# Where the first FFN's gated banks are emptied, and which stage sums the second FFN's shift and scale

## The chip, the core and the metric

The kernel runs on one core of one Trainium2 chip. The engines named here are TensorE (PE, matmuls and transposes into the eight PSUM banks), VectorE (DVE), ScalarE (ACT), GpSimd (POOL) and SyncE (SP), whose queue issues the weight loads. Each engine works through a list of instructions that is fixed when the kernel is built; it takes them in that order and waits where one is not ready. The metric is the device time of one execution in microseconds, the median of several runs.

## The reference

A decoder trunk of two layers over one sequence of 256 tokens, width 1024, all in float32. A vector `c` modulates every sub-layer: for each layer nine vectors of length 1024 come out of one product, and each of them is a shift, a scale or a gate.

```python
for l in range(DEPTH):
    mod = cond @ ada_w[l] + ada_b[l]
    (sh1, sc1, g1, sh2, sc2, g2, sh3, sc3, g3) = jnp.split(mod, N_MOD, axis=-1)
    n1 = modulate(rmsnorm(h, norm_ffn1[l]), sh1, sc1)
    h = h + MACARON_WEIGHT * g1[:, None, :] * swiglu(n1, ffn1_w_gu[l], ffn1_w_down[l])
    n2 = modulate(rmsnorm(h, norm_mix[l]), sh2, sc2)
    h = h + g2[:, None, :] * hybrid_mixer(n2, positions, ...)
    n3 = modulate(rmsnorm(h, norm_ffn2[l]), sh3, sc3)
    h = h + MACARON_WEIGHT * g3[:, None, :] * swiglu(n3, ffn2_w_gu[l], ffn2_w_down[l])
return rmsnorm(h, final_norm)
```

`swiglu` is silu of one half of `x @ w_gu` times the other half, then `@ w_down` (2816 hidden columns). `hybrid_mixer` projects the tokens once and runs three groups of heads, A (dilated windows), B (latent attention) and C (attention over the 64 best keys that an indexer picks for each token), and projects their joined outputs with `w_out`.

## The kernel before

**Products.** The 256 tokens are two tiles of 128 rows. A float32 product is made of three products of halves: `split` copies a weight into `hi` (ACT, L243) and subtracts that from the weight into `lo` (DVE, L244), activations are split likewise, and PE adds hi x hi, lo x hi and hi x lo (L196). Chunks of gated activations are called `chh` and `chl`.

**The stream of weights.** Every weight is in one stream in DRAM, in order of use. `load` (L225) issues it from SP's queue, mostly 1 MB at a time, into `raw`, which has three buffers. A buffer comes free when DVE has made its last `lo` from it, or its last sum (below). `hi` and `lo` have six buffers each; the weights of the last two down blocks go to larger ones, `xhi` and `xlo`.

**The stages.** Each layer is an FFN, the mixer and a second FFN. The first FFN of the first layer has 11 blocks of 256 hidden columns. `lead` does its first four (LEADB) at once, k by k, in all eight PSUM banks (four named `pb`, four named `pa`), while the weights and the modulation arrive. It then applies silu (ACT, L642) and the product (DVE, L644) to each bank, transposes the results on PE (L201, `pb<-ident,pr`) and copies them as chunks (ACT L709, DVE L710). Blocks 4 to 10 follow one by one in `block`: `gu_mm` for each of the two halves f, then `gu_act` (ACT, DVE, then POOL's product L721 and POOL's `chl` L723). The down products of the blocks run behind, by the table FIRST_DOWN, in the four `pa` banks: before block 4 the first of them already runs.

**The modulation vectors.** The class `Ada` makes one vector in four steps, each a load of 1 MB and two DVE instructions that add a column of `cond` times a part of it to `acc` (L433 for the first, L435 for the others). `acc` has one buffer, so the next vector cannot begin before the former is used up. At the end a gate (names with G) is split and spread over the partitions by PE with `ones_r`; a shift or scale (SH, SC) takes eight PE transposes into two banks (`pb<-ident,acc`) and two DVE reductions (L460). ADA_PLAN says which vectors are made in which stage (layer 0: first FFN, mixer, second FFN, then layer 1), and `Jobs.run` spreads the steps over the blocks of the FFN (7 parts) or over eight places `j0` to `j7` in the list STEPS of the mixer. SC2 and SH2 are needed by the mixer's norm, G2 at the mixer's end, SC3 and SH3 by the second FFN's norm.

**The mixer.** The indexer of group C finds its keys by a chain of DVE maxima (L938, L939) that ends in the mask `msk` (L942). Head A's score products (`pb<-k,q`) and softmax (`neg`, L1031; `pe`) run beside and after it. Then come C's scores, which begin with the mask (`pb<-msk,identr`), and the output projection (`pa<-hi,chh` and so on) with G2 at the end.

**The order.** A scheduler lists the instructions by a simulated time, with a priority (`tc.high_priority`) for the steps that hand chunks on. What it lists, the chip keeps.

## Time and profile before

| | us |
|---|---|
| median of three runs (1097.83, 1098.70, 1100.39) | 1098.70 |
| the profiled execution | 1097.09 |
| its span in the trace | 1095.2 |
| PE busy in the span | 1049.6 |
| DVE busy | 819.8 |
| ACT busy | 620.1 |
| POOL busy | 194.9 |

The stages of layer 0 lie at these times of the trace: `lead` until 64.7, blocks 4 to 10 of the first FFN until 234.3, the mixer until 372.2, then the second FFN. Rows of a profile give the busy time of an engine, the mean length of one instruction in ns (one can overlap the next, so starts can be closer together than lengths), and the idle time ahead of a group of instructions with its releaser, the engine and line that ended the wait. [...]

### The profile page before, as it was taken

What the parts mean: (1) busy time and instruction counts of PE and PEld (TensorE: products, weight loads), DVE (VectorE), ACT (ScalarE), POOL (GpSimd) and SP (SyncE); (2) the same over time, 40 slices, a digit from 0 to 9 for tenths busy, and PEclk for the clock granted to TensorE, in tenths of its full rate; (3) what the DMA queues carried; (4) which work ended last, traced back from release to release, by engine and by line L of the source; (5) the groups of instructions that cost most, each with busy time, mean ns of one, the idle gap of its engine ahead of it and who ended that gap; (6) DMA issues with size and microseconds to landing.
All of it is one profiled execution on the core that took longest, in us unless ns stands there. A gap on an engine that the chain in (4) does not pass through costs nothing.

```text
span 1095.2 us, 15506 instructions
## 1 busy us (share of the span) xinstructions
PE 1049.6 (96%) x5634; PEld 878.2 (80%) x5634; DVE 819.8 (75%) x1334; ACT 620.1 (57%) x1177; POOL 194.9 (18%) x211
## 2 busy tenths in 40 slices
PE   5999999789999999999999999999999999999997
PEld 3778877668887688888878888887788778888885
DVE  6987877886795787786889877886669757656563
ACT  5554534366666766455555555555676667555561
POOL 1002221122000022232311323131200001222231
PEclk9999999899999999999999999999999999999999
DMA  8978887865355188787848888783536516666541
GB/s 340 373 267 296 293 320 269 334 223 189 111 188 193 64 298 290 270 303 267 293 160 303 292 303 293 281 313 132 188 125 208 178 58 210 233 227 224 212 183 38
DMA packets 38988, 255.84 MB, mean 234 GB/s; under 512 B 4824, under 2 KB 5208, under 8 KB 11008
## 3 DMA queue, kind: packets, MB, share of 16 engines
q1 hardware_dynamic: 38160, 253.14, 63.4%
q0 software_dynamic: 752, 1.71, 0.4%
q8 instruction: 44, 0.72, 0.3%
q14 instruction: 32, 0.26, 0.1%
HBM read 253.76 MB, written 1.07 MB: 233 GB/s over the span
## 4 chain that ended last, share of the span: by engine, by line
PE 80%; issue 6%; DVE 4%; ACT 4%; DMA 3%; POOL 2%; SPq 0%; DVEq 0%; POOLq 0%; ACTq 0%
PE pb L196 41%; PE pa L196 36%; PE pb L201 3%; DMA raw<-in_stream_dram 2%; DVE lo L244 1%; ACT hi L243 1%; DVE up L657 1%; PE pa L201 1%; POOL pr L721 1%; DMA invt<-in_inv_dram 1%; DVE acc L435 1%; POOL chl L723 1%; DMA scr<-gtab 0%; ACT nT L533 0%; ACT z L533 0%
## 5 line engine op out<-in xcount | busy, mean ns | idle before, releaser
L244 DVE TENSOR_TENSOR lo<-raw,hi 128x1024 fp32r<-128x1024 f32 (+3 forms) x314 | 380.7, 1227 | 145.5 <-ACT hi L243 143.5
L243 ACT CAST hi<-raw 128x1024 fp32r<-128x1024 f32 (+3 forms) x314 | 317.7, 1034 | 200.7 <-PE pb L196 94.0
L196 PE MATMUL pb<-nT,hi 128*128 128x512 f32 x1184 | 420.1, 396 | 5.3 <-ACT hi L243 5.3
L196 PE MATMUL pb<-nT,lo 128*128 128x256 f32 x1184 | 333.1, 284 | 2.2 <-DVE lo L244 2.2
L196 PEld LDWEIGHTS pb<-nT,hi 128*128 128x128 f32 x1184 | 222.9, 189 | 56.5 <-ACT hi L243 6.8
L196 PEld LDWEIGHTS pb<-nT,lo 128*128 128x128 f32 x1184 | 224.0, 189 | 6.1 <-DVE lo L244 3.1
L435 DVE SCALAR_TENSOR_TENSOR acc<-raw,cond,acc 128x1024 f32<-128x1024 f32 x118 | 155.5, 1317 | 20.1 <-DMA raw<-in_stream_dram 18.0
L721 POOL TENSOR_TENSOR pr<-sil,pr 128x256 f32<-128x256 f32 x74 | 76.8, 1038 | 516.4 <-DVE pr L718 310.6
L196 PE MATMUL pa<-hi,chh 128*128 128x512 f32 x328 | 105.0, 396 | 0.0
L196 PE MATMUL pa<-lo,chh 128*128 128x512 f32 x328 | 104.6, 392 | 0.4 <-DVE lo L244 0.4
L196 PE MATMUL pa<-hi,chl 128*128 128x512 f32 x328 | 103.3, 393 | 0.0
L196 PE MATMUL pa<-hi,nT 128*128 128x512 f32 (+3 forms) x320 | 89.2, 368 | 2.5 <-ACT nT L561 1.6
L723 POOL TENSOR_TENSOR chl<-pr,chh 128x256 fp32r<-128x256 f32 x74 | 81.7, 1105 | 53.6 <-ACT chh L723 53.6
L196 PEld LDWEIGHTS pa<-lo,chh 128*128 128x128 f32 x328 | 61.6, 189 | 13.5 <-DVE lo L244 0.8
L196 PEld LDWEIGHTS pa<-hi,chl 128*128 128x128 f32 x328 | 61.5, 189 | 13.1 <-issue 0.3
L196 PEld LDWEIGHTS pa<-hi,chh 128*128 128x128 f32 x328 | 60.3, 189 | 13.9 <-ACT chh L723 0.9
L196 PEld LDWEIGHTS pa<-hi,nT 128*128 128x128 f32 x320 | 58.8, 188 | 12.4 <-ACT nT L561 2.2
L196 PE MATMUL pa<-nT,hi 128*128 128x256 f32 x352 | 67.2, 289 | 0.0
L723 ACT CAST chh<-pr 128x256 fp32r<-128x256 f32 x74 | 30.0, 406 | 50.0 <-POOL pr L721 49.6
L196 PE MATMUL pb<-hi,nT 128*128 128x512 f32 x160 | 49.7, 413 | 8.4 <-ACT hi L243 3.9
L196 PEld LDWEIGHTS pa<-nT,hi 128*128 128x128 f32 x352 | 54.7, 189 | 3.3 <-issue 3.1
L196 PE MATMUL pa<-lo,nT 128*128 128x512 f32 (+3 forms) x160 | 54.2, 367 | 0.0
(210 smaller groups left out, 1278.2 us busy)
## 6 DMA issues: line engine op xcount, KB each, us to landing
raw<-in_stream_dram SPq DMA_DIRECT2D x218, 1024.0 KB, 4.9
up<-in_stream_dram SPq DMA_DIRECT2D x16, 512.0 KB, 12.6
raw<-in_stream_dram SPq DMA_DIRECT2D x4, 976.0 KB, 4.7
raw<-in_stream_dram SPq DMA_DIRECT2D x4, 768.0 KB, 4.3
raw<-in_stream_dram SPq DMA_DIRECT2D x4, 640.0 KB, 4.0
brev<-scr POOLq DMA_DIRECT2D x3, 512.0 KB, 10.6
h<-in_x_dram SPq DMA_DIRECT2D x2, 512.0 KB, 4.1
raw<-in_stream_dram SPq DMA_DIRECT2D x2, 512.0 KB, 3.6
```

The source lines that it names most:

```text
L196: last_pe[0] = nc.tensor.matmul(*a, **k)
L201: last_pe[0] = nc.tensor.transpose(*a, **k)
L243: ia = S.copy(hi[:, :n], src)
L244: iv = V.tensor_sub(lo[:, :n], src, hi[:, :n].bitcast(F32))
L435: iv = V.scalar_tensor_tensor(self.acc, src, cond[:, k:k + 1], self.acc, op0=ALU.mult, op1=ALU.add)
L657: V.tensor_tensor_reduce(out=src, in0=src, in1=condb, op0=ALU.mult, op1=ALU.add, scale=scale, scalar=first, accum_out=dst)
L721: G.tensor_tensor(pr, sil, pr, op=ALU.mult)
L723: last = [S.copy(ch[0], pr), G.tensor_tensor(ch[1], pr, ch[0].bitcast(F32), op=ALU.subtract)]
```

## The change

In the first FFN `lead` only applies silu and the product, and writes the results into two large buffers, `prods`; transposes and chunk copies move into a new function, `lead_turn`. The weights of block 4 come ahead of the first down block's in the stream (`get_gu(LEADB)` before `load_dn(0)`), both its loads being issued before the four splits, which take them in turn. PE's work on the first half of block 4 stands directly behind `lead`; the four `lead_turn` calls and the load of down block 0 follow it, then the second half of block 4, then the down products as before. In ADA_PLAN SC3 and SH3 move from the first FFN to the mixer of layer 0, ahead of G2: 12 steps in the FFN where there were 20, and 12 in the mixer where there were four.

```diff
-ADA_PLAN = 'G1.SC2.SH2.SC3.SH3,G2,G3.1SC1.1SH1.1SC2,1SH2.1G1.1SC3.1SH3,1G2,1G3'
+ADA_PLAN = 'G1.SC2.SH2,SC3.SH3.G2,G3.1SC1.1SH1.1SC2,1SH2.1G1.1SC3.1SH3,1G2,1G3'
...
         def get_gu(b):
             if b not in gu_units_:
-                if b and (IO == 2 or IO == 1 and b == 1):
+                if first and b == LEADB:
                     r = [load(gu_unit(wgu, l, b, side)) for side in range(2)]
                     w = [split(r[i % 2][:, i // 2 * 1024:(i // 2 + 1) * 1024]) for i in range(4)]
                     gu_units_[b] = (w[0::2], w[1::2])
...
+            prods = [x4(nm("prods")) for _ in range(2)]
             with tc.high_priority(offset=HP):
                 for i in range(LEADB):
-                    pr = [row_act(p) for p in banks[i]]
-                    p = psB()
...
+                    for t, p in enumerate(banks[i]):
+                        c = (i % 2 * NT + t) * T
+                        row_act(p, prods[i // 2][:, c:c + T])
+            return prods
+
+        def lead_turn(prods, i):
+            with tc.high_priority(offset=HP):
+                p = psB()
+                for f in range(2):
+                    for t in range(NT):
+                        c = (i % 2 * NT + t) * T + f * P
+                        PE.transpose(p[:, (2 * f + t) * P:(2 * f + t + 1) * P], prods[i // 2][:, c:c + P], ident)
+                for f in range(2):
+                    if i == LEADB - 1:
+                        ch = [wk.tile([P, T], F32R, tag="pT", name=nm("cht"), bufs=PTB) for _ in range(2)]
+                    else:
+                        ch = chunk_tile()
+                    pf = p[:, f * T:(f + 1) * T]
+                    S.copy(ch[0], pf)
+                    V.tensor_sub(ch[1], pf, ch[0].bitcast(F32))
+                    act[2 * i + f] = ch
...
         if first:
-            lead()
+            prods = lead()
+            get_gu(LEADB)
             open_acc()
+
+            def between(i):
+                if i == 0:
+                    for j in range(LEADB):
+                        lead_turn(prods, j)
+                    load_dn(0)
+
+            block(LEADB, between)
             for b in range(LEADB, NB):
                 now = FIRST_DOWN[b]
-                load_dn(now[0])
-                get_gu(b)
+                if b > LEADB:
+                    load_dn(now[0])
+                    get_gu(b)
                 if now[0] < NB - SKEW:
                     down_block(now[0])
-                block(b)
+                if b > LEADB:
+                    block(b)
```

`block(b, between)` calls `between(f % 2)` after each half. The orders of the two kernels differ in the first FFN and in the mixer of layer 0 and nowhere else. Three places follow, each as it stands in one engine's list. Numbers in names count the tiles of a program, so the same tile has another number in the other kernel; in brackets stands whose semaphore an instruction waits for.

PE at the end of `lead`, before: the last `lo` products, then the transposes of the gated products `pr` and the first down product (`pa_594`).

```order
L196 MATMUL pa_183<-lo_477,nT_107 128x512
L201 MATMUL pb_518<-ident,pr_512 128x128 [waits DVE_49]
L201 MATMUL pb_518<-ident,pr_516 128x128 [waits DVE_49]
L201 MATMUL pb_518<-ident,pr_512 128x128
L201 MATMUL pb_518<-ident,pr_516 128x128
L201 MATMUL pb_539<-ident,pr_533 128x128 [waits DVE_49]
L201 MATMUL pb_539<-ident,pr_537 128x128 [waits DVE_49]
L201 MATMUL pb_539<-ident,pr_533 128x128
L201 MATMUL pb_539<-ident,pr_537 128x128
L201 MATMUL pb_560<-ident,pr_554 128x128 [waits DVE_49]
L196 MATMUL pa_594<-hi_600,chh_523 128x512 [waits Activation_49]
```

PE after the change, behind the first half of block 4 (`pb_560` and `pb_561` are its two banks): transposes of `prods`, then the first down product (`pa_556`).

```order
L196 MATMUL pb_561<-nT_107,lo_545 128x256
L201 MATMUL pb_619<-ident,prods_510 128x128 [waits DVE_49]
L201 MATMUL pb_619<-ident,prods_510 128x128 x3
L201 MATMUL pb_632<-ident,prods_511 128x128 [waits DVE_49]
L201 MATMUL pb_632<-ident,prods_511 128x128 x3
L201 MATMUL pb_645<-ident,prods_511 128x128 [waits DVE_49]
L201 MATMUL pb_645<-ident,prods_511 128x128 x3
L196 MATMUL pa_556<-hi_660,chh_611 128x512 [waits Activation_49]
L196 MATMUL pa_557<-hi_660,chh_611 128x512
```

The transposes no longer stand directly behind `lead`, and those into `pb_645` stand last before the down product.

DVE in the mixer, before: two sums of G2 and the `lo` halves ahead of the output projection, whose first is `lo_3255`.

```order
L435 SCALAR_TENSOR_TENSOR acc_2889<-raw_3298,cond,acc_2889 128x1024 [waits DMAHW1_49]
L435 SCALAR_TENSOR_TENSOR acc_2889<-raw_3298,cond,acc_2889 128x1024 [waits DVE_49]
L1040 RECIPROCAL sm_3017<-sm_3017 128x2 [waits Activation_49]
L1046 TENSOR_SCALAR pe_3020<-pe_3020,sm_3017 128x256 [waits DVE_49,PE_49]
L244 TENSOR_TENSOR lo_3215<-raw_3208,hi_3214 128x1024 [waits Activation_49]
L244 TENSOR_TENSOR lo_3255<-raw_3252,hi_3254 128x1024 [waits DMAHW0_49,Activation_49]
L244 TENSOR_TENSOR lo_3259<-raw_3252,hi_3258 128x1024 [waits Activation_49]
L244 TENSOR_TENSOR lo_3303<-acc_2889,hi_3302 128x1024 [waits PE_49,Activation_49]
L1079 TENSOR_TENSOR chl_3143<-pb_3137,chh_3142 128x256 [waits Activation_49]
L244 TENSOR_TENSOR lo_3345<-raw_3342,hi_3344 128x1024 [waits DMAHW2_49,PE_49,Activation_49]
```

DVE after the change, at the same place: the `lo` of other output weights, four sums of G2 and then `lo_3245`, the one that the first output product reads.

```order
L244 TENSOR_TENSOR lo_3197<-raw_3194,hi_3196 128x1024 [waits DMAHW5_49,Activation_49]
L244 TENSOR_TENSOR lo_3201<-raw_3194,hi_3200 128x1024 [waits Activation_49]
L1062 RECIPROCAL sm_3223<-sm_3223 128x2 [waits Activation_49]
L435 SCALAR_TENSOR_TENSOR acc_3187<-raw_3190,cond,acc_3187 128x1024 [waits DMAHW4_49,DMASW0_49,Pool_49]
L1062 RECIPROCAL sm_3233<-sm_3233 128x2 [waits Activation_49]
L1068 TENSOR_SCALAR pe_3226<-pe_3226,sm_3223 128x256 [waits DVE_49]
L435 SCALAR_TENSOR_TENSOR acc_3187<-raw_3190,cond,acc_3187 128x1024 [waits DVE_49]
L1068 TENSOR_SCALAR pe_3236<-pe_3236,sm_3233 128x256 [waits DVE_49]
L435 SCALAR_TENSOR_TENSOR acc_3187<-raw_3204,cond,acc_3187 128x1024 [waits DMAHW6_49,DVE_49]
L435 SCALAR_TENSOR_TENSOR acc_3187<-raw_3204,cond,acc_3187 128x1024 [waits DVE_49]
L244 TENSOR_TENSOR lo_3245<-raw_3242,hi_3244 128x1024 [waits DMAHW7_49,Activation_49]
L244 TENSOR_TENSOR lo_3249<-raw_3242,hi_3248 128x1024 [waits Activation_49]
```

The first output product's `lo` now stands behind four sums and two other `lo`; SH3's eight sums are done a few rows earlier (the last is row 440 of this list).

PE in the mixer, before: the last products of A's values (`pT,vA`) among C's masked scores, and the first output products.

```order
L196 MATMUL pb_3222<-msk_2280,identr 128x256
L196 MATMUL pb_3223<-msk_2280,identr 128x256
L196 MATMUL pb_3222<-k_2814,q_2813 128x256
L196 MATMUL pb_3184<-pT_3135,vA_2696 64x256 [waits Activation_49]
L196 MATMUL pb_3184<-pT_3129,vA_2696 64x128
L196 MATMUL pb_3184<-pT_3135,vA_2696 64x128
L196 MATMUL pb_3223<-k_2814,q_2813 128x256
L196 MATMUL pa_3218<-hi_3254,chh_3142 128x512 [waits Activation_49]
L196 MATMUL pa_3219<-hi_3254,chh_3142 128x512 [waits PE_49]
L196 MATMUL pa_3218<-lo_3255,chh_3142 128x512 [waits DVE_49]
L196 MATMUL pa_3219<-lo_3255,chh_3142 128x512
```

PE after the change: SH3's transposes, C's masked scores, and the first output product.

```order
L201 MATMUL pb_3174<-ident,acc_2992 128x128 [waits DVE_49]
L201 MATMUL pb_3174<-ident,acc_2992 128x128 x3
L201 MATMUL pb_3180<-ident,acc_2992 128x128 x4
L196 MATMUL pb_3212<-msk_2211,identr 128x128 [waits PE_49]
L196 MATMUL pb_3212<-k_2750,q_2749 128x128
L196 MATMUL pb_3212<-msk_2211,identr 128x256
L196 MATMUL pb_3212<-k_2750,q_2749 128x256
L196 MATMUL pb_3213<-msk_2211,identr 128x128 [waits DVE_49]
L196 MATMUL pb_3213<-k_2750,q_2749 128x128
L196 MATMUL pb_3213<-msk_2211,identr 128x256
L196 MATMUL pb_3213<-k_2750,q_2749 128x256
L196 MATMUL pa_3208<-hi_3244,chh_3103 128x512 [waits Activation_49]
```

The eight transposes of `acc_2992` now stand ahead of the masked scores and the output products.

## Rows read from the trace of the kernel before

**Rows 1.** The page: busy time of an engine, share of the span, instructions.

```profile
PE 1049.6 (96%) x5634; PEld 878.2 (80%) x5634; DVE 819.8 (75%) x1334; ACT 620.1 (57%) x1177; POOL 194.9 (18%) x211
```

**Rows 2.** Stages: length, busy time of PE, PEld, DVE, ACT, POOL; clock, DMA share, GB/s.

```profile
98.20:234.30 136.10, 124.21 (x616) 101.87 (x615) 111.30 (x143) 63.12 (x102) 29.68 (x33) 0.95 0.81 302
234.30:372.20 137.90, 135.50 (x840) 112.22 (x841) 101.90 (x274) 90.92 (x224) 8.86 (x16) 1.00 0.45 160
378.00:480.00 102.00, 102.00 (x540) 87.38 (x539) 81.43 (x97) 58.69 (x97) 23.32 (x20) 1.00 0.76 274
```

**Rows 3.** What PE waited for from 98.2 to 234.3: total us, times, longest.

```profile
PE pb L196 <- ACT hi L243: 5.3, 3, 2.7
PE pa L196 <- POOL chl L723: 2.3, 3, 1.3
PE pb L196 <- DVE lo L244: 2.2, 2, 1.5
PE pa L196 <- ACT chh L723: 1.6, 1, 1.6
```

**Rows 4.** What SP's queue waited for from 98.2 to 234.3, same columns.

```profile
SPq L225 <- DVE lo L244: 40.4, 10, 7.8
...
SPq L225 <- DVE acc L435: 20.1, 8, 2.8
```

**Rows 5.** DVE by line, 98.2 to 234.3: busy us, mean ns, idle before.

```profile
L244 DVE TENSOR_TENSOR lo<-raw,hi 128x1024 fp32r<-128x1024 f32 (+1 forms) x35 | 42.9, 1256 | 12.3 <-ACT hi L243 11.7 <-POOL chl L723 0.6
L435 DVE SCALAR_TENSOR_TENSOR acc<-raw,cond,acc 128x1024 f32<-128x1024 f32 x29 | 37.7, 1302 | 1.8 <-DMA raw<-in_stream_dram 1.4
L460 DVE TENSOR_REDUCE modc<-pb 128x4 f32<-128x512 f32 x8 | 5.2, 685 | 2.9 <-PE pb L201 2.8
...
L433 DVE TENSOR_SCALAR acc<-raw,cond 128x1024 f32<-128x1024 f32 x4 | 3.0, 744 | 0.0
```

**Rows 6.** Shorter stretches, columns as in rows 2.

```profile
68.00:72.50 4.50, 4.50 (x19) 3.61 (x17) 3.85 (x10) 1.77 (x6) 0.00 (x0) 0.62 0.68 237
...
160.00:200.00 40.00, 34.85 (x172) 28.53 (x170) 30.52 (x34) 17.70 (x28) 7.23 (x8) 0.96 0.75 284
200.00:213.00 13.00, 8.50 (x32) 6.51 (x33) 10.36 (x13) 6.67 (x8) 1.70 (x3) 0.61 0.83 312
```

**Rows 7.** PE by line, 98.2 to 234.3: transposes of sums.

```profile
L201 PE MATMUL pb<-ident,acc 128*128 128x128 f32 x32 | 4.5, 288 | 0.0
```

**Rows 8.** PE in order of time at the end of lead: start, length, idle before.

```profile
67.73 0.85 PE L201 MATMUL pb<-ident,pr 128*128 128x128 f32 x4 [2.51 <-DVE pr L644]
```

**Rows 9.** The page: ACT's casts of weights, busy and mean ns, idle before.

```profile
L243 ACT CAST hi<-raw 128x1024 fp32r<-128x1024 f32 (+3 forms) x314 | 317.7, 1034 | 200.7 <-PE pb L196 94.0
```

**Rows 10.** POOL in order of time: a product beside and without DVE sums.

```profile
196.87 1.70 POOL L721 TENSOR_TENSOR pr<-sil,pr 128x256 f32<-128x256 f32 x1 [21.21 <-DVE pr L718]
...
200.24 0.73 POOL L721 TENSOR_TENSOR pr<-sil,pr 128x256 f32<-128x256 f32 x1
```

**Rows 11.** The mixer's end in two stretches, columns as in rows 2.

```profile
322.00:340.00 18.00, 18.00 (x126) 15.09 (x126) 14.34 (x37) 15.68 (x38) 1.56 (x2) 1.00 0.69 262
340.00:372.00 32.00, 31.22 (x158) 23.60 (x157) 16.95 (x45) 17.87 (x46) 0.28 (x1) 1.00 0.28 99
```

**Rows 12.** PE in order of time, mixer: scores, masked scores, first output products.

```profile
321.87 1.36 PE L196 MATMUL pb<-k,q 64*128 64x128 f32 x11
...
337.50 0.44 PE L196 MATMUL pb<-msk,identr 128*128 128x128 f32 x2
...
340.77 0.74 PE L196 MATMUL pa<-hi,chh 128*128 128x512 f32 x2
```

**Rows 13.** DVE in order of time, mixer: the first softmax pair, and what follows.

```profile
322.82 0.29 DVE L1031 CUSTOM_DVE_ANT_0 neg<-pb,biasm 128x128 f32<-128x128 f32 x1 [0.81 <-PE pb L196]
...
323.38 1.22 DVE L244 TENSOR_TENSOR lo<-raw,hi 128x1024 fp32r<-128x1024 f32 x1
```

**Rows 14.** The page: loads of raw, KB each, median us to landing.

```profile
raw<-in_stream_dram SPq DMA_DIRECT2D x218, 1024.0 KB, 4.9
```

More of the change, by code (lines that the diff above doesn't have):

```diff
@@ L638, in gu_rows, with row_act @@
             return row_act(p)
-        def row_act(p):
+        def row_act(p, pr=None):
             sil = three("neg", name=nm("sil"))[:, 0:T]
             S.activation(sil, p[:, 0:256], AF.Silu)
-            pr = three("pe", name=nm("pr"))[:, 0:T]
+            if pr is None:
+                pr = three("pe", name=nm("pr"))[:, 0:T]
             V.tensor_tensor(pr, sil, p[:, 256:512], op=ALU.mult)
@@ L695, in lead @@
                     ws[k + 1] = split_unit(raws[k + 1][2], 2048)
+            prods = [x4(nm("prods")) for _ in range(2)]
             with tc.high_priority(offset=HP):
                 for i in range(LEADB):
-                    pr = [row_act(p) for p in banks[i]]
-                    p = psB()
-                    for f in range(2):
-                        for t in range(NT):
-                            PE.transpose(p[:, (2 * f + t) * P:(2 * f + t + 1) * P], pr[t][:, f * P:(f + 1) * P], ident)
-                    for f in range(2):
-                        if i == LEADB - 1:
-                            ch = [wk.tile([P, T], F32R, tag="pT", name=nm("cht"), bufs=PTB) for _ in range(2)]
-                        else:
-                            ch = chunk_tile()
-                        pf = p[:, f * T:(f + 1) * T]
-                        S.copy(ch[0], pf)
-                        V.tensor_sub(ch[1], pf, ch[0].bitcast(F32))
-                        act[2 * i + f] = ch
+                    for t, p in enumerate(banks[i]):
[18 more added lines that the diff above has]
+                    act[2 * i + f] = ch
         def gu_act(ps2, f):
@@ L740, in rows_act, with block @@
                     V.tensor_sub(act[f][1], p[:, 0:T], act[f][0].bitcast(F32))
-        def block(b):
+        def block(b, between=None):
             for f in (2 * b, 2 * b + 1):
@@ L747, in block @@
                     prior[:] = gu_act(p, f)
+                if between:
+                    between(f % 2)
         def load_dn(b):
```

## The prediction, made before the change was run

> **What bounds the kernel now.** Read the busy shares first: TensorE (PE) works 96% of the span [rows 1], so a gain has to come out of the stretches where it does not work, or works at the lower of its two clocks. The table by stage [rows 2] shows where that is. In the first FFN from 98.2 to 234.3 us PE is busy 124.21 of 136.10 us at a mean clock of 0.95; in the first mixer, 234.3 to 372.2, it is busy 135.50 of 137.90 at 1.00; in the second FFN it never rests. So the first FFN is the stage that waits and the first mixer is not. In the first FFN PE waited for a weight's high half from ACT (5.3 us), for POOL's chl (2.3), for the low half from VectorE (DVE) (2.2) and for ACT's chh (1.6) [rows 3]: weights came late. They came late because SP, which issues every load into three buffers, was itself waiting for DVE to empty them, 40.4 us for `lo` and 20.1 us for `acc` [rows 4]. DVE is busy 111.30 of the 136.10 us there. The sums of the modulation vectors hold 33 of its instructions: 29 of 1.30 us and 4 of 0.74 [rows 5]. The second FFN shows the same kind of block at DMA share 0.76 and 274 GB/s without a gap [rows 2]; the first runs at 0.81 and 302.
>
> **FFN, what leaves.** The plan takes SC3 and SH3 out: 8 loads of 1 MB, 16 sums (2 of 0.74 and 14 of 1.30, 19.7 us of DVE), 4 reductions of 0.69 us and 16 transposes. At 302 GB/s the 136.1 us moved 41.1 MB; without 8.4 it is 32.7, and over a stage shortened by the 17.1 us found below that is 275 GB/s, what the second FFN takes without a gap [rows 2]. The gaps lie late in the stage, where loads come closer than on the mean; that is the reason for a lower end. So I count the idle of the late blocks as gone except what POOL's chl at 221 to 225 holds, 1.7 us: 136.10 less 124.21 is 11.9 us of idle time [rows 2], less 1.7 is 10.2. With the gaps goes the lower clock: 200 to 213 shows 0.61 [rows 6], that is 0.78 of 13 us at the lower level, PE busy in 8.50 of 13, so 0.78 x 8.50 / 2 = 3.3 us lost; 160 to 200 shows 0.96, so 0.08 x 34.85 / 2 = 1.4. The 16 transposes are 16 x 0.14 = 2.2 us (32 of them took 4.5 [rows 7]). Sum: 10.2 + 3.3 + 1.4 + 2.2 = 17.1. Ends: 13 if two of the larger gaps (1.6 and 2.7) stay, 20 if everything goes. I take 17.1.
>
> **The hand-over.** Before, PE stands 2.51 us at 65.2 because its second set of transposes waits for the gated product L644 [rows 8], and then works at 0.62 from 68.0 to 72.5 [rows 6]: 3.4 us at the lower level, 1.7 lost; 4.2 together. After the change PE goes straight into the first half of block 4, whose weights lie first in the stream and whose high and low halves stand in the same places of the ACT and DVE lists as the first down block's did. That gap goes. But the transposes of the last product need a bank that block 4 has just filled: `pb_645` waits until DVE's second addition has read `pb_561`. On DVE two `lo` and a sum (1.2 + 1.2 + 1.3 us) stand ahead of that addition, and on ACT a cast of 1.03 [rows 9]. By these prices the transposes come about 2 us late. Behind them the first down matmul waits for a cast which on ACT stands behind one that waits for POOL's product and then its own, 0.73 us alone and 1.70 beside DVE [rows 10]: about 1.5 us more. 3.5 us of waiting, again followed by the lower clock, replaces 4.2. I count it at nothing; ends are -3 (the lists slip less) and +2.
>
> **The mixer, what comes.** 16 sums, 8 loads, 4 reductions, 16 transposes. The 8 sums of SC3 stand in the place of 6 of G2's ahead of the mask, where none of them is now inside the chain of maxima; I take them as free. The trouble is behind it. Before, DVE did 2 sums between the mask and the end; now it does SH3's 8 and G2's 8. It had room, 3.7 us from 322 to 340 and 15.1 from 340 to 372 [rows 11], but its list is fixed and in order, and the room lies late. Call s the first `k,q` pair after the mask, 321.87 before [rows 12]; DVE's `neg` starts 0.95 later [rows 13].
> SH3 shares one accumulator with SC3, so its first sum cannot start before SC3 is transposed, just behind s. From `neg` to SH3's last sum the list holds 4 softmax pairs (0.56 us each from start to start [rows 13]: 2.2), the 8 sums (0.74 + 7 x 1.30 = 9.8), one `lo` (1.2), two reductions (1.4) and a dozen small rows (2.5): 17.1. So the last sum ends at s + 18.0. PE reaches SH3's transposes after the work that took 321.87 to 337.50 before, 15.6 us [rows 12], and waits 2.4.
> Then comes the larger wait. The first output matmul needs `hi_3244` and `lo_3245`. On DVE ahead of `lo_3245` stand, after the last sum, reductions, two softmax pairs and small rows (3.8), `lo_3197` and `lo_3201` (2.4), four sums of G2 (5.2) and small ones (0.8): 12.2. The load has a path of its own: its buffer is free after `lo_3201`, at 6.2; it lands 4.9 later [rows 14], and ACT casts 1.03: 12.1. Both paths end together, so neither can be blamed alone. PE has about 3.5 us of transposes and mask work in that time, and so stands 8 to 9 us. The output projection begins at s + 18.0 + 12.1 = s + 30.1; before it began at 340.77, s + 18.9 [rows 12]: +11.2. What follows is as before (from 340.77 to 372.2). Two gaps of over 2 us are each followed by the lower clock as the one at 65 us was, 1.7 each: 3.4. Sum: 11.2 + 3.4 = 14.6. Ends: 9 (no clock loss, two sums hidden) and 20 (the loads behind the parked buffers land 3 us late as well, and the short matmuls of the last heads run at the lower clock).
>
> The trace shows 1.7 us lost behind one gap of 2.51 us [rows 6, 8], and I count that loss once for the hand-over and once for each wait in the mixer. [...]
>
> **Sum.** -17.1 + 0 + 14.6 is -2.5 us. The profiled execution took 1097.09 (span 1095.2), 1.6 below the median of the three runs, 1098.7; I put the change against the median: 1096.2. Its own range, with 13 to 20 and 9 to 20 not at their ends together, is 1092 to 1101. About 0.2%, 2.2 us, is what a measurement of this kernel can tell from no change.
>
> **Rivals.**
> A, the mixer hides most of it. DVE's idle time from 322 to 372 is 18.7 us [rows 11], nearly the 18 us of new sums. If ACT and the loads run far enough ahead of it that only half of the 12 us before the first output matmul is exposed, and the first wait vanishes, the mixer loses 6: 1098.7 - 17.1 + 6 = 1087.6. Against it: the list is in order, and 12.2 us of DVE rows stand in front of that one `lo`.
> B, slower: three buffers and one accumulator. Two loads of SH3 lie in two of the three buffers until SC3 is transposed, so the output weights come last and one behind the other. At 3.5 us per load in a row (1.05 MB at 302 GB/s [rows 2]) the third lands 2 to 3 us later than one alone; with the small matmuls after it at the lower clock the mixer loses 20. If then the first FFN keeps the two larger gaps, since the late blocks' loads come closer than the mean, it gives only 14: 1098.7 - 14 + 20 = 1104.7. It decides as soon as the mixer's loss is 2.2 above the FFN's gain. For it speaks that all terms of the mixer wait on one another.
> C, the FFN does not get faster: the stream itself is the limit there, not DVE, and the gaps shrink only by the 8 loads' share, -8; with the mixer's 14.6 it is 1105.3. Against it: the second FFN without any gap, and SP's waits, which name DVE.
>
> **How the numbers follow.** Forecast 0.53, A 0.15, B 0.25, C 0.07. The forecast lies near the bound of faster, so it splits: 0.27 faster, 0.20 same, 0.06 slower. A is faster; B is 0.06 same and 0.19 slower; C is slower. Together faster 0.42, same 0.26, slower 0.32. The range runs from A's time to B's.
>
> **What the profile after would show.** PE without waits from 150 to 215, clock 1.00 there and the first FFN some 17 us shorter (end near 217): the first term. A PE gap behind transposes of `prods` instead of the one in front of them: the hand-over. In the mixer a gap of about 2 us before `ident,acc`, then 8 to 9 us before the first `hi,chh` of the output, the releaser DVE `lo` or ACT `hi`, the clock near 0.6 behind it, and a stage of about 153 us instead of 138: the mixer. A mixer gap under 5 us makes A right; gaps left in the FFN at 200 us make B or C right. I am wrong in kind if the difference lies in another stage, since the lists differ nowhere else.

## The result and the profile after

The changed kernel is slower: median 1104.43 us (1101.56 to 1107.56, 8 runs) against 1098.29 for the kernel before in the same runs, a ratio of 1.0053 (95% interval 1.0035 to 1.007). The profiled execution took 1104.54 us, span 1102.7; before it was 1097.09 and 1095.2.

TensorE is busy 1.4 us more than in [rows 1]; the other 6.1 us of the longer span are idle time. From the page of the changed kernel:

```profile
PE 1051.0 (95%) x5634; PEld 880.5 (80%) x5634; DVE 821.4 (74%) x1334; ACT 619.6 (56%) x1177; POOL 199.9 (18%) x211
```

The first FFN ends with the first transpose of the mixer's norm (`ident,z`), at 219.74 us instead of 234.26: 14.5 us earlier. Its two stretches answer to the first line of [rows 2] and have its columns (length, busy time of PE, PEld, DVE, ACT, POOL; clock, DMA share, GB/s):

```profile
98.00:150.00 52.00, 52.00 (x269) 43.64 (x269) 37.57 (x56) 28.11 (x44) 13.20 (x14) 1.00 0.81 295
150.00:219.70 69.70, 66.99 (x337) 55.69 (x335) 54.96 (x66) 34.46 (x58) 18.91 (x17) 0.98 0.72 260
```

Idle time there is 2.7 us instead of 11.9, the clock 0.98 where [rows 6] had 0.61 at 200 to 213. The mixer takes it back. It runs to the next `ident,z`, which is at 373.38 before and at 381.00 after: 139.12 us against 161.26, +22.1. What lies behind the mixer kept its length (721.8 and 721.7), so -14.5 + 22.1 is the 7.5 us of the spans, up to 0.1 of rounding and rest.

The mixer by its own steps: to the first `k,q` after the mask (s: 321.87 before, 308.76 after), to the first output product, to the end. The kernel before, then after, same columns:

```profile
234.26:373.38 139.12, 136.24 (x843) 112.51 (x843) 102.66 (x276) 91.60 (x226) 9.36 (x16) 1.00 0.44 159
...
321.87:340.77 18.90, 18.90 (x129) 15.52 (x129) 15.24 (x39) 16.33 (x40) 1.56 (x2) 1.00 0.67 255
340.77:373.38 32.61, 31.35 (x159) 23.71 (x158) 17.10 (x45) 17.99 (x47) 0.99 (x1) 1.00 0.27 97
```
```profile
219.74:381.00 161.26, 143.21 (x858) 117.54 (x859) 123.87 (x299) 91.77 (x226) 12.11 (x18) 0.94 0.52 189
...
308.76:340.46 31.70, 21.64 (x145) 17.61 (x144) 26.71 (x62) 16.34 (x47) 1.55 (x2) 0.81 0.65 239
340.46:381.00 40.54, 36.45 (x157) 26.92 (x158) 25.84 (x44) 19.29 (x41) 2.46 (x3) 0.90 0.49 190
326.01:331.47 5.46, 5.45 (x20) 3.36 (x20) 2.29 (x8) 2.88 (x6) 1.55 (x2) 0.70 0.73 259
340.46:346.00 5.54, 5.54 (x14) 4.36 (x15) 5.47 (x5) 0.90 (x1) 0.00 (x0) 0.56 0.95 359
363.38:370.00 6.62, 3.91 (x27) 2.86 (x28) 1.10 (x5) 4.26 (x15) 0.00 (x0) 0.74 0.00 0
```

Up to s it is 1.4 us longer (89.02 less 87.61), from s to the first output product 12.8 (31.70 less 18.90), behind that 7.9 (40.54 less 32.61). Idle time grew by 15.2 us (18.05 less 2.88) and busy time by 7.0. Of those 7.0, the 16 transposes are 1.6 (0.41, 0.36 and 0.85 from their starts to the next product); the last three lines, each behind a wait, give 0.30 x 5.45 + 0.44 x 5.54 + 0.26 x 3.91 = 5.1 us of lower clock; C's masked scores at the end, shown below, are 1.3 more; and up to s PE's work is 0.9 shorter. The records show the lower clock as half of the higher: the share granted to PE reads 0.50 from 340.40 to 345.00 in the changed kernel, and in the kernel before 0.50 from 68.5 to 71.0, with 1.00 from 67 to 68 and from 71.5 to 75. In the kernel before, products of 128x512 start 0.42 to 0.43 us apart in the stretch at 0.50 and 0.22 to 0.24 in the one at 1.00 behind it. From these two, a stretch at a mean clock of m is put down, as an estimate, as losing 1 - m of its busy time; the halves in the forecast count alike. The idle time has four names. PE's waits from 220 to 381 us (total us, times, longest):

```profile
PE pa L196 <- ACT hi L243: 9.0, 1, 9.0
PE pb L201 <- ACT pe L1066: 2.7, 1, 2.7
PE pb L201 <- POOL iqq L851: 2.1, 1, 2.1
PE pb L201 <- DVE acc L435: 1.1, 1, 1.1
```

The longest one can be followed link by link. DVE, and then ACT, of the changed kernel (start, length, instruction, idle time before it and releaser):

```profile
331.50 0.29 DVE L1053 CUSTOM_DVE_ANT_0 neg<-pb,biasm 128x128 f32<-128x128 f32 x1 [2.06 <-PE pb L196]
...
332.06 2.35 DVE L244 TENSOR_TENSOR lo<-raw,hi 128x1024 fp32r<-128x1024 f32 x2
...
337.37 2.60 DVE L435 SCALAR_TENSOR_TENSOR acc<-raw,cond,acc 128x1024 f32<-128x1024 f32 x2
340.44 2.36 DVE L244 TENSOR_TENSOR lo<-raw,hi 128x1024 fp32r<-128x1024 f32 x2 [0.47 <-ACT hi L243]
```
```profile
328.57 1.99 ACT L243 CAST hi<-raw 128x1024 fp32r<-128x1024 f32 x2 [3.21 <-DMA raw<-in_stream_dram]
...
335.79 0.40 ACT L1066 ACTIVATE pe<-pe,sm 128x128 f32<-128x128 f32 x1 [0.86 <-DVE sm L1062]
339.37 1.99 ACT L243 CAST hi<-raw 128x1024 fp32r<-128x1024 f32 x2 [3.18 <-DMA raw<-in_stream_dram]
```

The high halves were cast by 330.6, but the low halves stand in DVE's list behind a softmax row that waited 2.06 us for PE, then at the lower clock (0.50 from 328.5 to 331.4). They ended at 334.41, which freed the buffer; the next load landed at 339.37, 5.0 later; its first cast ended at about 340.4 and PE started at 340.46. DVE's list was through with G2's four sums at 339.97 and stood 0.47 us for that cast. The two paths of the forecast do end within half a microsecond of each other. A third one ends 3.2 us before the load: ACT's list was through with its softmax rows at 336.2 and then stood idle until the load came.

The 2.7-us wait near the mixer's end can be read from PE's list. The kernel before, then after:

```profile
354.41 0.33 PE L196 MATMUL pb<-msk,identr 128*128 128x128 f32 x2
...
356.16 0.87 PE L201 MATMUL pb<-ident,pe 128*128 128x128 f32 x6
356.79 0.70 PE L196 MATMUL pa<-hi,chh 128*128 128x512 f32 x2
...
359.64 1.14 PE L201 MATMUL pb<-ident,pe 128*128 128x128 f32 x9
```
```profile
357.80 0.73 PE L196 MATMUL pa<-hi,chh 128*128 128x512 f32 x2
...
360.67 0.22 PE L196 MATMUL pb<-msk,identr 128*128 128x128 f32 x1
...
362.18 1.20 PE L201 MATMUL pb<-ident,pe 128*128 128x128 f32 x9
366.09 1.54 PE L201 MATMUL pb<-ident,pe 128*128 128x128 f32 x6 [2.71 <-ACT pe L1066]
```

Before, C's last two heads have their masked scores together in 1.75 us, and 2.85 us of output products stand between these scores and the last transposes; their softmax runs meanwhile, and nothing waits. After, the scores come one head at a time, about 1.5 us each (the three heads take 4.5 us where they took 3.3), and the same output products stand ahead of the last of them. Nothing but nine transposes is left to do during its softmax. No run puts this order back alone. Of the runs below, e2 and e14 keep it and have 2.71 us again; in e9 output products follow the last scores, and the wait is 0.6.

At the hand-over the transposes now wait, and the down product behind them. PE, and the stretches around it:

```profile
73.04 0.66 PE L201 MATMUL pb<-ident,prods 128*128 128x128 f32 x4 [2.27 <-DVE pr L727]
75.53 1.14 PE L196 MATMUL pa<-hi,chh 128*128 128x512 f32 x2 [1.83 <-ACT chh L718]
```
```profile
64.70:70.80 6.10, 6.07 (x40) 5.27 (x38) 5.58 (x10) 4.05 (x10) 0.00 (x0) 1.00 0.97 368
70.80:73.70 2.90, 0.66 (x4) 0.42 (x4) 2.90 (x4) 0.65 (x3) 0.56 (x1) 1.00 0.19 68
73.70:75.50 1.80, 0.00 (x0) 0.00 (x0) 0.86 (x2) 1.07 (x4) 1.28 (x2) 1.00 0.76 282
75.50:78.00 2.50, 2.47 (x6) 2.01 (x7) 1.95 (x6) 1.55 (x5) 0.51 (x1) 0.53 1.01 419
78.00:80.00 2.00, 2.00 (x8) 1.54 (x8) 0.32 (x1) 0.00 (x0) 0.00 (x0) 0.73 0.63 262
```

4.1 us of waiting stand where [rows 8] had 2.51, and 0.47 x 2.47 + 0.27 x 2.00 = 1.7 us of lower clock follow, as before.

### The profile page after: what moved, and what is told of

The parts are those of the page before. It is cut to its first block, busy times and chain, and to the rows that moved or that the text cites. A ratio compares the mean times of both kernels' runs of the same rounds, so it can differ in the third digit from the quotient of the medians.

```text
span 1102.7 us, 15495 instructions
## 1 busy us (share of the span) xinstructions
PE 1051.0 (95%) x5634; PEld 880.5 (80%) x5634; DVE 821.4 (74%) x1334; ACT 619.6 (56%) x1177; POOL 199.9 (18%) x211
## 4 chain that ended last, share of the span: by engine, by line
PE 70%; ACT 3%; DVE 2%; issue 1%; DMA 0%; POOL 0%; DVEq 0%; POOLq 0%
PE pb L196 37%; PE pa L196 29%; PE pb L201 2%; PE pa L201 1%; ACT hi L243 1%; DMA raw<-in_stream_dram 0%; DVE lo L244 0%; ACT nT L533 0%; ACT z L533 0%; POOL ss L335 0%; ACT pT L1082 0%; ACT z L489 0%; DVE acc L435 0%; DVE work L961 0%; ACT qkB L1112 0%
```

## The experiments

Stage lengths are read from one profiled execution each, which is up to 4.2 us off the median of its kernel (e6); ratios come from timed runs against the kernel before on the same chip. The mixer's length repeats well where its plan is the same (139.12 and 139.15 in before and e1, 161.26 and 161.39 in after and e2). The end of the first FFN does not: nine profiles with the new plan and the new hand-over lie between 216.4 and 223.0. What lies behind the mixer is 721.7 to 725.0 us, 728.5 in e11. "Output" is the first output product, counted from the mixer's start; "tail" is the rest of the mixer. Ratios of kernels that leave work out are in brackets.

| kernel | ratio (95% interval) | FFN ends | output | tail | mixer |
|---|---|---|---|---|---|
| before | 1 | 234.26 | 106.51 | 32.61 | 139.12 |
| after | 1.0053 (1.0035 to 1.007) | 219.74 | 120.72 | 40.54 | 161.26 |
| e1 | 1.0000 (0.9988 to 1.0012) | 235.30 | 106.56 | 32.59 | 139.15 |
| e2 | 1.0041 (1.0024 to 1.0058) | 216.17 | 120.21 | 41.18 | 161.39 |
| e3 | 1.0053 (1.0035 to 1.0072) | 220.77 | 120.11 | 38.46 | 158.57 |
| e4 | 1.0111 (1.0084 to 1.0139) | 229.21 | 116.60 | 36.93 | 153.53 |
| e5 | 1.0098 (1.0072 to 1.0124) | 216.41 | 109.50 | 57.53 | 167.03 |
| e6 | 1.0028 (1.0010 to 1.0047) | 222.99 | 108.62 | 48.65 | 157.27 |
| e7 | 1.0008 (0.9987 to 1.0029) | 219.34 | 107.61 | 50.87 | 158.48 |
| e8 | 1.0037 (1.0016 to 1.0057) | 216.89 | 109.73 | 51.72 | 161.45 |
| e9 | [1.0019 (1.0004 to 1.0035)] | 219.06 | 117.09 | 39.84 | 156.93 |
| e10 | [1.0171 (1.0154 to 1.0188)] | 217.44 | 115.05 | 57.42 | 172.47 |
| e11 | 1.0131 (1.0106 to 1.0156) | 219.95 | 117.05 | 39.90 | 156.95 |
| e12 | 0.9984 (0.9969 to 1.0000) | 217.26 | 108.51 | 44.97 | 153.48 |
| e13 | 1.0042 (1.0020 to 1.0064) | 217.69 | 115.12 | 44.15 | 159.27 |
| e14 | [1.0008 (0.9994 to 1.0022)] | 218.55 | 112.83 | 41.62 | 154.45 |

**Each half of the change alone.** e1 is the changed kernel with the old plan; e2 is the kernel before with the new one.

```diff
-ADA_PLAN = 'G1.SC2.SH2,SC3.SH3.G2,G3...
+ADA_PLAN = 'G1.SC2.SH2.SC3.SH3,G2,G3...
```

> The new hand-over with the old plan (SC3 and SH3 back in the first FFN). Theory 1 (the whole loss comes from the mixer, the hand-over is worth little): the mixer stays at its 139 us from the first transpose of its norm to that of the next, PE waits about 4.1 us behind the first half of block 4 instead of 2.5 in front of the transposes, the late gaps of the first FFN stay, and the time is within 3 us of before: 1098 to 1101. Theory 2 (the hand-over helps, the plan eats it): 1093 to 1096. Theory 3 (the new order of loads itself costs): 1102 or more.

> The old hand-over with the new plan (SC3 and SH3 in the mixer). Theory 1: the mixer is as long as in the changed kernel, 161 us against 139, with the same wait of about 9 us before the first output product; the first FFN is 15 to 17 us shorter than before; 1102 to 1106, and the effects of the two parts add up. Theory 2 (the hand-over is the larger loss): 1097 to 1100.

With the old plan the new hand-over changes nothing that can be measured. The plan alone carries the loss, and its mixer has the same four waits as the changed kernel (8.9, 2.7, 2.2, 1.2 us). Its FFN gains 18.1 us, more than the whole change does.

**The lower clock.** e3 puts 36 products that nobody reads behind C0's scores, so that PE works through the 9-us wait.

```diff
+            if l == 0 and i == 0:
+                m = last_pe[0]
+                for n in range(36):
+                    r = PE.matmul(acc[0][0], identr, nT[2][:, n % KD]..., start=True, stop=True)
+                    if n == 0:
+                        after(r, m)
```

> The changed kernel with 36 useless products of 512 columns behind the first masked scores of the mixer of layer 0, into a bank that the first output product overwrites, so that PE works through most of its 9 us wait; nothing of the result changes. Theory 1 (of the mixer's 22 us some 2 to 3 are output products at the lower clock behind that wait): the clock is at its higher level when the output projection begins, and the time is 2 to 3 us under the changed kernel's, about 1102. Theory 2 (only the wait itself counts): no change, 1104. Theory 3 (the useless products outlast the wait): 1105 or more.

The stretch from 322 to 341, with a mean clock of 0.66 in the changed kernel, then reads in e3:

```profile
322.00:341.00 19.00, 17.59 (x97) 13.24 (x96) 16.36 (x29) 7.75 (x20) 1.56 (x2) 1.00 0.79 294
```

The mixer is 2.7 us shorter, the time the same within the intervals: the clock did what the first theory said, the time what the second said. The clock behind that wait costs no more than about 2.7 us; most of the loss is the wait itself.

**Fewer sums in the mixer.** e4 leaves SC3 in the FFN (`'G1.SC2.SH2.SC3,SH3.G2,...'`).

> The changed kernel with only SH3 in the mixer, SC3 back in the first FFN: four loads and eight sums are moved instead of eight and sixteen. SH3's sums end before the mask is made, so no second vector has to wait for the one accumulator; six of G2's sums stand ahead of the first output product's low half where there were two before and twelve sums of both vectors in the changed kernel. Theory 1 (the price in the mixer is what stands behind the mask in DVE's list, and is not proportional): the mixer loses 5 to 8 us, the first FFN gains 10 to 13, 1092 to 1096. Theory 2 (each vector costs the mixer 11 us and gives the FFN 7): 1101 to 1103.

The FFN gives back two thirds of its gain (5.0 instead of 14.5) while the mixer still loses 14.4: half of the sums cost well over half of the loss. There are waits of 3.2 (`ident,pe`), 2.4 (`hi,chh`) and 2.1 us (`iqq`), and C's masked scores begin 9 us later in the mixer than before (112.3 us after its start, 103.2 before). Neither theory gave the time, 1109.5: a first FFN that gained only 5 and a mixer that lost 14 were in neither.

**Moving the wait.** In the mixer's list of steps, e5 prepares the output weights before the sums that follow the mask; e6 also puts the last modulation step behind C2; e7 is e6 with the old hand-over; e8 is e7 with step j1 moved off the position rotation. The lines are e6's.

```diff
-... 'm0', 'j5', 'p2', 'j6', 'z0', 'C0', 'p0', 'w0', 'p1', 'w2', 'w1', 'j7', 'p3', 'w3', 'C4', 'p4', 'C2', 'w4'
+... 'm0', 'p2', 'p0', 'j5', 'z0', 'C0', 'w0', 'p1', 'w2', 'j6', 'w1', 'p3', 'w3', 'C4', 'p4', 'C2', 'j7', 'w4'
```

> The changed kernel with only the order of steps in the mixer of layer 0 altered: the two loads of output weights come before SH3's last load, and G2's second step behind the second group of output products, so that in DVE's list the low half which the first output product reads stands ahead of SH3's last two sums and of all of G2's. Theory 1 (the 9 us wait is the price of sums standing ahead in DVE's list and of the loads behind them, not of DVE's total work): the wait is gone or under 2 us and the output projection begins 108 to 111 us into the mixer instead of 120.7; some 4 us come back as a wait for G2's gate, because all of its sums still have to end before the scores that stand behind it; 1095 to 1098. Theory 2 (DVE has too much work behind the mask in any order): the wait moves, the mixer stays within 3 us of 161, 1102 or more.

> The kernel of the run before, with G2's last step behind the last scores as well. Theory 1: the wait for the gate goes too, the mixer is 146 to 150 us long, 1090 to 1093, faster than both the changed kernel and the kernel before by more than 0.2%. Theory 2: as above, 1102 or more.

> The old hand-over with the new plan and the order of steps of the run before. If the two parts add up as the first runs show (the plan alone was 2.4 us under both parts, and its first FFN ended 3.6 us earlier in the trace), it is 2 to 4 us faster than the run before: 1087 to 1090. If the new hand-over only lost because the mixer was the bound behind it, it is within 1 us of the run before.

> The kernel of the run before, with SC3's second step moved behind the third top-k round, so that no sum runs on DVE while POOL turns the indexer's queries. Theory 1 (POOL's products took 1.34 and 1.41 us instead of 0.35 and 0.51 because DVE's sums ran beside them): the 2.1 us wait of PE for iqq is gone, POOL's two instructions are back at 0.35 and 0.52, and unless the sums that now lie between the maxima make the mask late, the time falls by about 2 us. Theory 2 (POOL is late for another reason): the wait stays.

The output projection comes back to 107.6 to 109.7 us, nearly where it was before, and the wait reappears at the broadcast of the gate G2 (`hi,ones_r`), whose sums are now last: 9.8 us in e5, 7.8 in e6, 9.2 in e7 and e8. Moving the step moves the wait and hardly shortens it: the mixers of 146 to 150 us of e6's first theory did not come. e7 is still faster than the changed kernel (1.0008 against 1.0053, intervals apart). In e8 the rotation no longer makes PE wait, but 3.9 us before `ident,pe` take that place, the mask ends 4.6 us later in the mixer than in e7, and the whole is slower than e7.

**List or buffers?** e9 cuts the sums of SC3, SH3 and G2 of layer 0 to 8 of their 1024 columns and keeps every load; e10 does the reverse, leaves out the 12 loads and sums over another tile. Both leave that work out of the computation.

```diff
+                if l == 0 and v in (SC3, SH3, G2):
+                    src, to = src[:, 0:8], to[:, 0:8]
```
```diff
+            idle = l == 0 and v in (SC3, SH3, G2)
+            raw = None if idle else load(ada_unit(l, v, i))
```

> The changed kernel with the sums of SC3, SH3 and G2 of layer 0 cut to 8 of 1024 columns (the rest of each vector is left at zero), so that 24 sums of 1.3 us become short ones; every load, transpose and reduction stays. Theory 1 (DVE's work and its fixed list make the mixer longer): the wait before the output projection goes, the mixer is 139 to 145 us long, 1084 to 1089. Theory 2 (the loads and the three buffers that they occupy make it longer): the mixer stays above 152 us, 1095 or more.

> The changed kernel with the 12 loads of SC3, SH3 and G2 of layer 0 left out; their sums run at full size on the residual rows, which lie in SBUF, so that DVE does the same work on the wrong numbers. Theory 1: DVE's work remains, the mixer stays at 153 to 161 us, 1097 to 1104. Theory 2: the mixer falls to 150 us or less, 1094 or less.

In e9 the other three waits shrink to 0.6 us or vanish, and the 9-us wait stays. The list came out in another order at the mixer's end (above), so the 2.7-us wait did not go by the sums' time alone. PE's waits, ACT and DVE in e9:

```profile
PE pa L196 <- ACT hi L243: 9.1, 1, 9.1
```
```profile
324.07 1.99 ACT L243 CAST hi<-raw 128x1024 fp32r<-128x1024 f32 x2 [0.68 <-DMA raw<-in_stream_dram]
...
335.05 1.99 ACT L243 CAST hi<-raw 128x1024 fp32r<-128x1024 f32 x2 [4.26 <-DMA raw<-in_stream_dram]
```
```profile
327.63 2.36 DVE L244 TENSOR_TENSOR lo<-raw,hi 128x1024 fp32r<-128x1024 f32 x2
```

The pair before lands at 324.07, its low halves, behind softmax rows in DVE's list, end at 329.99, the next load lands 5.1 us later and is cast: the buffer chain makes the wait without the sums, and the mixer stays above 152 us as the second theory said. e10 says little on the other path, since its lists came out in another order: the first output products stand ahead of C's masked scores, which begin 17 us later in the mixer than in the changed kernel, and the wait (10.9 us) stands at the gate. Its mixer of 172.5 us lies outside both theories.

e11 gives the sums two accumulators, paid for with one `lo` buffer (6 to 5).

> The changed kernel with two accumulators for the vectors instead of one, and five buffers for low halves instead of six to make room. SH3's sums no longer wait until SC3 is transposed, and in DVE's list all of SH3's sums and four of G2's stand ahead of the mask. If the one accumulator is what makes the mixer long, it shortens by 8 us or more, to 153 or less (1097 or less, apart from what the missing buffer costs the other stages). If DVE's work is what counts, the mask only comes later instead, the mixer stays within 5 us of 161, and the time is 1101 or more.

The 9-us wait is gone and the mixer 4.3 us shorter, short of the 8 that the one accumulator was to be worth; the mask ends 26 us later, as the other reading said, because 18 of the 24 sums now stand ahead of it. It is the slowest full version, with waits before `ident,pe` in several heads and 6.8 us lost outside both stages. The missing `lo` buffer is the only other edit; that it is the cause there was not tried alone.

**Both paths taken apart.** e13 loads the first output weights into two tiles of their own, so that they wait for no raw buffer; e14 adds e9's cut to it, and so leaves those sums out.

```diff
+                if l == 0 and ci == 0:
...
+                    for i in range(2):
+                        t = x4(nm("raw"))
+                        SY.dma_start(t, src[:, i * 1024:(i + 1) * 1024])
+                        wo[i] = split(t)
```

> The changed kernel, with one thing altered: the first output weights of the first mixer (the pair p0) are loaded into two tiles of the eight-fold set of their own, 1024 columns each, instead of a raw buffer, so that their load need not wait for the buffer of the pair before (in the changed kernel: lo of that pair ends at 334.4, load 5.0 us, cast 1.0 us, first output product at 340.5 after 9.0 us of waiting). The vector engine's list also comes out in another order: the low parts of p0 stand straight behind those of the pair before, ahead of the scale's sums. Theory 1 (the buffer chain carries the wait once the low parts stand ahead of the sums): the casts of p0 follow those of the pair before at about 330.5, the wait before the first output product falls from 9.0 us to 0 to 3 us, the first output product comes 112 to 115 us into the mixer (120.7 in the changed kernel). Theory 2 (the sums hold the mixer by their mere time on the vector engine, wherever they stand): the wait comes back behind the first output product, at the gate or the other low parts, and the mixer keeps at least 158 of its 161.3 us; by theory 1 alone it would fall to 153 to 156 and the time to 1097 to 1100 us.

> As e13_own_buffer, and the sums of the second FFN's shift, scale and gate (SC3, SH3, G2) cut to 8 of their 1024 columns, with all loads kept; this leaves the rest of those sums out. With the sums alone cut (e9) the 9.1-us wait stayed, on the buffer chain. If list and buffer chain are the only two arms, both gone here, the wait before the first output product is under 2 us, the first output product comes 106 to 110 us into the mixer (106.5 in the kernel before) and the mixer takes 141 to 147 us. If a third arm (the landing of the weights at a full DMA share, since SC3's and SH3's six loads of 1 MB remain) holds it, a wait of 3 us or more on a cast or a DMA stays there and the mixer stays above 150 us.

In e13 the 9-us wait is 0.3, with 1.1 before the first low half, but 4.7 us appear before SH3's transposes, because its last sums now wait for their load, which stands behind the new loads in SP's list. The first output product comes 5.6 us earlier, as theory 1 said, and the mixer is only 2.0 shorter, as theory 2 said. But theory 2's reason, the sums' time, is not shown: what came back is the late load, and behind the first output product 1.0 us more of idle time and 2.6 more of PE work, at a mean clock of 0.84 instead of 0.90. PE's waits, and DVE's line for those sums:

```profile
PE pb L201 <- DVE acc L435: 4.7, 1, 4.7
PE pb L201 <- POOL iqq L851: 2.1, 1, 2.1
...
PE pa L196 <- DVE lo L244: 1.1, 1, 1.1
```
```profile
324.90 2.60 DVE L435 SCALAR_TENSOR_TENSOR acc<-raw,cond,acc 128x1024 f32<-128x1024 f32 x2 [1.17 <-DMA raw<-in_stream_dram]
```

In e14, without the sums' time and without the chain, 4.9 us of the wait are left. ACT in e14, then its whole mixer and two stretches of it (columns as above):

```profile
327.76 0.73 ACT L1069 ACTIVATE pe<-pe,sm 128x128 f32<-128x128 f32 x2
328.40 3.87 ACT L243 CAST hi<-raw 128x1024 fp32r<-128x1024 f32 x4
```
```profile
218.55:373.00 154.45, 142.88 (x858) 117.78 (x859) 101.16 (x299) 92.28 (x226) 11.73 (x19) 0.96 0.54 198
331.38:337.40 6.02, 6.02 (x15) 4.67 (x16) 3.90 (x9) 0.89 (x1) 0.00 (x0) 0.55 0.74 276
354.54:362.00 7.46, 4.75 (x32) 3.45 (x32) 1.46 (x5) 5.08 (x15) 0.00 (x0) 0.77 0.00 0
```

The four casts wait for no load: they stand behind the softmax rows in ACT's list, and two of them belong to the other pair. So there is a third path, ACT's order, behind the two of the forecast, and it is not the one that was expected: no load was late.

**The gate where it is used.** e12 is e7 with G2's broadcast held back until the first products of the last output chunk.

```diff
-                self.finish()
+                if l == 0 and v == G2:
+                    late.append(self)
+                else:
+                    self.finish()
...
+                if late:
+                    late.pop().finish(r[-1])
```

> The old hand-over with the new plan and the output projection first, as in the run with the old hand-over, and with G2's products with ones held back until the first part of the last output products is issued, so that PE works on instead of waiting 9.2 us for the gate; only the residual sums wait for it. Theory 1 (the wait for the gate is a place in PE's list and not a need): the wait is 0 to 3 us, the mixer 149 to 153 us instead of 158, 1090 to 1094. Theory 2 (DVE's list is late by as much for the residual): the wait only moves to the end of the mixer, 1097 to 1100.

The longest wait left in its mixer is 2.7 us. It has the lowest ratio: faster than the changed kernel, and against the kernel before 0.9984 with an interval that just reaches 1. Its mixer is 5.0 us shorter than e7's, which differs in this one thing; the intervals of the two whole kernels overlap. Its mixer still takes 14.4 us more than before, and its FFN gains 17.0.

## Why the prediction was wrong

The forecast was 1096.2, about the same or faster, with 1092 to 1101 as its own range; the time is 1104.4, outside that and on the other side. It lies inside the wide range only because rival B's time, 1104.7, is its end.

- **FFN, what leaves: right.** 17.1 us were forecast for the plan; e2, which has the plan alone, gained 18.1, and the four profiles with the new plan and the old hand-over gained 16.9 on the mean. Clock 0.98 and 2.7 us of idle time from 150 on are what was to be seen.
- **Hand-over, counted at nothing: wrong by about 2 us.** The place and the two waits were named, but they add up to 4.1 us, not 3.5, and the lower clock behind them costs 1.7, which that 3.5 did not contain; it was set against 4.2 that did. By these rows it is 4.1 + 1.7 - 4.2 = 1.6. FFN ends with the new hand-over and the whole new plan average 219.2 us (nine profiles, 216.4 to 223.0), with the old one 217.4 (four, 216.2 to 219.3): 1.8 us, though the two overlap. Ratios go the same way (e6 to e7, after to e2), with overlapping intervals. The size, between 0 and 3 us, is not settled.
- **Mixer, 14.6 forecast, 22.1 measured: the term that decided.** By its steps: the 8 sums of SC3 "as free" cost 1.4 before s, where PE now waits 2.1 us for `iqq`; from s to the output 12.8 against 11.2 and one lower clock of 1.7, 12.9; behind it 7.9 against the other 1.7. The excess is 1.4 - 0.1 + 6.2 = 7.5 us. That the middle step came out is in part luck: its waits are 1.06 and 9.00, 0.9 us less than the 2.4 and 8.6 that its sum holds, PE's work about as much more; its lower clock, 1.6, was right. The step that failed is "what follows is as before", with one lower clock of 1.7 us, which ended the account at the first output product. In its place the trace has 7.9 us: idle time that grew from 1.26 to 4.09 us, almost all of it the new wait of 2.7 before `ident,pe`; 2.4 us of lower clock behind the 9-us wait and 1.0 behind the new one; and 1.3 for C's scores taken one head at a time (0.3 is left). What followed was not as before, and PE's list shows it.
- **"Neither can be blamed alone": right by the trace, tested on one side.** The paths ended 0.47 us apart. With the sums' time gone (e9) the buffer chain alone held the wait at 9.1 us. The other side, the sums' place in DVE's list without the chain, no run shows: e13 takes the chain away, but with it the output weights' low halves move ahead of the sums of G2. The mixer, 22.1 us too long, is 2.0 shorter in e13, 4.3 in e9 and 6.8 in e14; each of the three has other waits in the place of those that went. That a third path stood behind the two was not foreseen.
- **The slow piece behind a wait.** The forecast counted one for the hand-over and one for each of two waits in the mixer, all at the 1.7 us lost behind the gap of 2.51 in [rows 6, 8]. The profile has one slow stretch behind the hand-over's two waits: 1.00 from 70.8 to 75.5 and 0.53 from 75.5 to 78, so none behind the first wait, of 2.27 us. In the mixer three waits have one, the third being the wait of 2.7 us that was not forecast, and by the estimate above they cost 1.6, 2.4 and 1.0 us. Not all waits of over 2 us have one: behind the 2.13 us before `ident,iqq` the clock is 1.00 (219.7 to 285.5).
- **Rival B** gave the time (1104.7, with 14 and 20 for the two stages), but not for its reasons. Its 14 in the first FFN was to come from gaps that stay; the gaps went, and 2.7 us of idle time were left. Its lower clock over small products is in the profile (0.74 from 363.38 to 370.00). Its own mechanism, output weights landing 2 to 3 us late behind parked loads, is not shown: the deciding load landed 5.0 us after its buffer was free, against 4.9 in [rows 14].

The 15.3 us left in e14's mixer, sums and chain being gone, are by its rows 8.7 of idle time (waits of 4.9, 2.7 and 1.9 us above all), 1.6 of transposes and 0.45 x 6.02 + 0.23 x 4.75 = 3.8 of lower clock behind two of the waits. 1.2 remain; C's scores stand one head at a time there too.

## What to carry to other kernels

Work taken off a stage with gaps and put into one without them has to be followed to that stage's end, not to the first wait: here a third of the loss came behind the last step that had been worked out, and the order that made part of it stood in PE's list before the run. Where several in-order lists meet in one wait, taking one away shortens little (of 22.1 us too many, 2.0 in e13 and 4.3 in e9); put the moved work where its result is first used, as e12 does with the gate, and look at which list is next. A lost wait and the wait that replaces it are to be priced alike, both with the clock behind them.

## What the hardware showed that was not expected

POOL's rotation of the indexer's queries slowed down beside DVE's sums. The changed kernel's POOL and DVE, then POOL in the kernel before, where one sum began 0.2 us after the second of them:

```profile
258.73 1.34 POOL L850 TENSOR_TENSOR tab<-iqq,sinf 128x80 f32<-128x80 f32 x1
260.15 1.41 POOL L851 TENSOR_TENSOR iqq<-tab 128x160 f32<-128x160 f32 x1
```
```profile
258.44 2.74 DVE L435 SCALAR_TENSOR_TENSOR acc<-raw,cond,acc 128x1024 f32<-128x1024 f32 x2 [4.62 <-DMA raw<-in_stream_dram]
```
```profile
273.12 0.36 POOL L828 TENSOR_TENSOR tab<-iqq,sinf 128x80 f32<-128x80 f32 x1
273.55 0.52 POOL L829 TENSOR_TENSOR iqq<-tab 128x160 f32<-128x160 f32 x1
```

The two instructions took 1.9 us more, and PE waited 2.1 us for `iqq` where it had not waited before. The wait is gone, and the two instructions take 0.35 and 0.52 us, where the sums are 8 columns wide (e9) and where they stand elsewhere (e8). In the changed kernel each of the two is longer by 0.9 to 1.0 us, less than the 1.3 of one sum, and the second ends 0.4 us after the second sum (261.56 and 261.18), within its own length of 0.5. By what path a sum slows them, no run shows.
